# Two reorderings and a final norm summed over features on all partitions, in a one-core decoder layer

## Chip, cores and metric

The kernel runs on one core of a Trainium2 chip. The metric is the device time of one execution in microseconds; the median of three runs is given. The engines are named as in the profile: PE (TensorE, the matrix engine), DVE (the vector engine), ACT (the scalar engine), POOL (GpSimd) and SP, whose queue issues nearly all DMAs.

## What is computed

One layer of a hybrid decoder on 1,024 prompt tokens with 16 meta tokens ahead of them, and on 64 new tokens (8 sequences of 8): 1,104 columns in all, of which the 16 meta columns are dropped behind the attention. Everything is float32, width 1,024. Cut to what matters here:

```
u  = rmsnorm(h, norm_mix)
z  = u @ w_in + b_in                    # 48 tiles of 128 outputs
h += (gated sum of pooling, convolution and attention branches) @ w_out
u2 = rmsnorm(h, norm_mlp)
h += square(relu(u2 @ w_up)) @ w_down   # 1024 -> 4096 -> 1024
y  = rmsnorm(h, norm_final)

def _rmsnorm(x, g):
    y = x32 * lax.rsqrt(jnp.mean(x32 * x32, axis=-1, keepdims=True) + NORM_EPS)
    return y * g
```

The outputs are y and the new states of the three branches.

## The kernel before

Features lie on partitions (8 tiles of 128) and tokens on columns. Each float32 product is made of three matmuls in a faster type: both operands are split into a high part (ACT copies it: `whi`, `uh`, `oph`) and a low part (DVE subtracts: `wlo`, `ul`, `opl`), and high x high, high x low and low x high are summed in one PSUM bank. The engines' lists are written out by hand in Python order (`manual_schedule`): each engine runs its instructions in the order in which the code issues them, and waits for semaphores.

Three places matter.

**The head.** The columns of x come in three chunks `CH` of 416, 320 and 368 columns. The first five tiles of w_in (`NHEAD`) run their products on chunk 0 before the norm is known, and scale afterwards. `proj_mm(ti, ci)` is the product of tile ti on chunk ci, 24 matmuls into a bank from `pmain`; `proj_chunk(ti, ci, ps)` takes it out of the bank again (DVE `un`, L903, then ACT), which frees the bank. The sixth call of `pmain` uses the bank of the first. `norm1(ci)` is the norm of a chunk as six steps: steps 0 and 1 square (ACT, L304) and add (DVE, L306); step 2 sums over the features with one-column matmuls, which puts tokens on partitions (PE L260), takes the reciprocal root (`rstd_cols`: DVE, ACT, DVE) and makes diagonal matrices of it (DVE L266); step 3 broadcasts those diagonals to all partitions with a matmul (PE L271); steps 4 and 5 scale and split. n1 is that list for chunk 1, n2 for chunk 2.

**The seam.** The MLP's two products are done with a Strassen-like scheme: 16 pairs of up products with 7 steps each, then 7 down products (`NPROD`), each over 4 output pairs mp and 2 halves hf. Up results ca and cb leave the banks on DVE or ACT, are squared, combined (`op_steps`: the differences d) and stored to DRAM. `op_load(n, q)` loads operand q of down product n back (SP's queue; four buffers rotate), `op_split(n, q)` splits it into oph (ACT) and opl (DVE). Operands 0 to 3 are read by the first half hf = 0 of a down product's pairs, 4 to 7 by hf = 1. In the last up pair (j = 15), step i splits operand i; step 5 also splits the second piece of down weights (`W.split_to(2)`, then `W.flush()` for wlo). Step 6 of the up products writes the bank that step 4's cb empties.

**The tail.** The last down product runs over 288 and then 256 columns. `final(srcs, a, c, last)` is the last norm over columns a to c. With `last` it has three steps: f0 (sums with tokens on partitions, reciprocal root on 128x2, diagonals), pre (ACT scales two of the eight tiles by norm_final), f3 (broadcast, copy to SBUF, eight scaled outputs, stores).

Of the kernel before, what the change touches and what calls it, by code (L numbers as in the profile page):

```python
# [7 lines left out]
F32 = mybir.dt.float32  # L8
# [106 lines left out]
def hybrid_trunk_kernel(ctx, tc, I, O):  # L115
# [61 lines left out]
    one = pool.tile([P, 4], F32, name="one", tag="st", bufs=8)  # L177
    V.memset(one, 1.0)
    A.activation(one, one, AF.Sqrt)
    X = [[None] * 8 for _ in CH]  # L180

    def load_x(ci, k0=0, k1=8):
# [37 lines left out]
    def col(off):  # L220
        return vec[:, off:off + 1]
# [657 lines left out]
    def proj_mm(ti, ci):  # L879
        kind, j = TILES[ti]  # L880
        wh, wl = wts[ti][:2]
        a, c = CH[ci]
        if kind in "qz" and ci == 0:
            a = NM
        ps = pmain()
        mm3(ps[:, :c - a], wh, wl, [(k, (Uh[k][:, a:c], Ul[k][:, a:c])) for k in range(8)])
        return ps
# [206 lines left out]
    n2 = norm1(2)  # L1094
    proj_open(4)
    b0_.append(proj_mm(4, 0))
    n1[2]()
    n2[0]()
    n2[1]()
    proj_chunk(3, 0, b0_[3])  # L1100
    b1_ = [proj_mm(0, 1)]
    proj_chunk(4, 0, b0_[4])
    b1_.append(proj_mm(1, 1))
    n1[3]()
    n2[2]()
    b1_.append(proj_mm(2, 1))
    proj_chunk(0, 1, b1_[0])
    proj_chunk(1, 1, b1_[1])
    n2[3]()
# [434 lines left out]
    def op_load(n, q):  # L1544
        if n < NPROD:
            ld[n, q] = page2("ld")
            SP.dma_start(ld[n, q][:, :L], opD[DORD[n][1], q])

    def op_split(n, q):
        if n < NPROD:  # L1550
            t = ld.pop((n, q))
            h, l = BD[n, q] = page("oph", F32R), page("opl", F32R)
            split(h[:, :L], l[:, :L], t[:, :L])
# [27 lines left out]
    for s in range(7 * NPAIR):  # L1581
# [41 lines left out]
        if j == NPAIR - 1:  # L1623
            for n in range(2):
                BC.pop((BX[i], n))
            if i < 5:
                op_split(0, i)
                op_load(0, i + 2)
            elif i == 5:
                op_split(0, 5)  # L1630
                op_split(0, 6)
                op_load(1, 0)
                op_load(1, 1)
            if i == 1:
                W.split_to(1)
                W.flush()
            elif i == 4:
                W.load_to(3)
            elif i == 5:
                W.split_to(2)  # L1640
                W.flush()
# [80 lines left out]
    def final(srcs, a, c, last):  # L1722
# [25 lines left out]
        def pre(ms):  # L1748
            for m in ms:
                h = H[m][:, a:c]  # L1750
                A.activation(h, h, AF.Copy, scale=col(V_NF + m))

        def f3():
            b = px2()
            bcast_tokens(b, box["r"], w)
            s = page("fbc")
            A.activation(s[:, :w], b[:, :w], AF.Copy)
            t = [page("fo")[:, :4 * w].rearrange("p (m c) -> p m c", m=4) for _ in range(2)]
            for m in range(8):
                h, o = H[m][:, a:c], t[m // 4][:, m % 4]  # L1760
                if m in (2, 5):
                    G.tensor_tensor(o, h, s[:, :w], ALU.mult)
                else:
                    V.scalar_tensor_tensor(o, h, col(V_NF + m), b[:, :w], ALU.mult, ALU.mult)
                if m in (0, 1, 3, 5, 7):
                    n = 2 if m > 1 else 1
                    (A if m in (1, 5) else SP).dma_start(
                        O["y"][m + 1 - n:m + 1, :, a:c].rearrange("m p c -> p m c"),
                                 t[m // 4][:, m % 4 + 1 - n:m % 4 + 1])
        idle = lambda: None  # L1770
        if last:
            return [f0, lambda: pre((2, 5)), f3]
        return [f0, idle, idle, idle, f1, idle, idle] + [f2(m) for m in range(8)]

    WD = {}
# [1 line left out]
    for n in range(NPROD - 1):  # L1777
        for mp in range(4):
# [3 lines left out]
            for hf in range(2):  # L1782
# [2 lines left out]
                W.split_to(i + 2)  # L1785
                W.flush()
                q = 2 * mp + hf
                op_split(n + 1, q)
                if q < 6:
                    op_load(n + 1, q + 2)  # L1790
# [185 lines left out]
```

## Time and profile before

| | us |
|---|---|
| median of 3 runs (lowest, highest) | 1661.78 (1661.28, 1661.79) |
| the profiled execution | 1662.0 |
| its span, first to last instruction | 1660.1 |
| PE busy | 1642.7 (99%) |
| DVE busy | 1134.5 (68%) |
| ACT busy | 750.5 (45%) |
| POOL busy | 5.8 |
| moved by DMA | 250.78 MB, 151 GB/s on the mean |

Busy shares are of the span. A matmul's record is longer than the distance to the next one, since matmuls overlap; where the text counts matmuls, it goes by their starts. A float32 matmul of the norms (not split into three) leaves two records. "PEclk" is the share of TensorE's full clock that was granted: 1.00 is 2.4 GHz, 0.50 is 1.2 GHz.

### The profile page before, as it was taken

How to read it: one execution, taken by the hardware profiler on the slowest of the kernel's cores; microseconds unless marked ns; L12 is line 12 of the kernel's file. 1: busy time of each engine (PE TensorE's matmuls, PEld its weight loads, DVE VectorE, ACT ScalarE, POOL GpSimd, SP SyncE). 2: the span in 40 equal slices, each digit the busy share in tenths (PEclk: the TensorE clock that was granted, in tenths of full speed). 3: DMA queues.
4: the chain of work that ended last, by engine and by line, in shares of the span. 5: the costliest groups of instructions: out<-in, count | busy, mean ns of one | idle time of the engine just before them, and what ended most of it. 6: DMA issues, size and time to landing. Idle time of an engine off the chain costs nothing.

```text
span 1660.1 us, 28943 instructions
## 1 busy us (share of the span) xinstructions
PE 1642.7 (99%) x11568; PEld 1618.2 (97%) x11568; DVE 1134.5 (68%) x2120; ACT 750.5 (45%) x1428; POOL 5.8 (0%) x14
## 2 busy tenths in 40 slices
PE   9999999999999999999999999999999999999997
PEld 8999999999999999999999999999999999999997
DVE  7786767867776666455584687777777844457674
ACT  6537667467675342364243343233332533333341
POOL 0000000000000000000000000000000000000000
PEclk9999999999999999999999999999999999999998
DMA  6051221231225353344253447777776955556652
GB/s 207 15 110 52 71 79 42 68 77 41 81 63 173 97 197 113 104 184 146 80 172 124 152 162 242 244 237 246 243 241 227 323 194 184 183 184 222 204 173 85
DMA packets 132123, 250.78 MB, mean 151 GB/s; under 512 B 33459, under 2 KB 64148, under 8 KB 131988
## 3 DMA queue, kind: packets, MB, share of 16 engines
q1 hardware_dynamic: 131428, 248.45, 46.2%
q8 instruction: 91, 1.49, 0.4%
q10 hardware_dynamic: 560, 0.48, 0.1%
q14 instruction: 44, 0.36, 0.1%
HBM read 168.52 MB, written 80.36 MB: 150 GB/s over the span
## 4 chain that ended last, share of the span: by engine, by line
PE 95%; DVE 2%; ACT 1%; DMA 1%; issue 0%; SPq 0%; DVEq 0%; ACTq 0%
PE pm L151 13%; PE pm L153 13%; PE pm L152 13%; PE m L1663 7%; PE m L1665 7%; PE m L1667 7%; PE m L1470 6%; PE m L1473 6%; PE m L1472 6%; PE pn L151 3%; PE pn L153 3%; PE pn L152 3%; PE px L634 2%; PE px L622 2%; PE qk L581 2%; PE px L271 1%
## 5 line engine op out<-in xcount | busy, mean ns | idle before, releaser
L151 PE MATMUL pm<-uh,whi 128*128 128x320 f32 (+3 forms) x1008 | 338.5, 336 | 0.6 <-ACT uh L342 0.5
L153 PE MATMUL pm<-uh,wlo 128*128 128x320 f32 (+3 forms) x1008 | 333.1, 330 | 0.0
L152 PE MATMUL pm<-ul,whi 128*128 128x320 f32 (+3 forms) x1008 | 332.2, 330 | 0.6 <-DVE ul L343 0.6
L1663 PE MATMUL m<-oph,whi 128*128 128x272 f32 (+2 forms) x896 | 258.5, 289 | 0.0
L1665 PE MATMUL m<-opl,whi 128*128 128x272 f32 (+2 forms) x896 | 258.0, 288 | 0.0
L1667 PE MATMUL m<-oph,wlo 128*128 128x272 f32 (+2 forms) x896 | 257.8, 288 | 0.0
L93 ACT ACTIVATE whi<-wraw 128x1024 fp32r<-128x1024 f32 (+1 forms) x127 | 130.0, 1025 | 205.6 <-PE m L1665 138.3
L94 DVE TENSOR_TENSOR wlo<-wraw,whi 128x1024 fp32r<-128x1024 f32 (+1 forms) x127 | 150.6, 1187 | 98.3 <-ACT whi L93 98.3
L151 PEld LDWEIGHTS pm<-uh,whi 128*128 128x128 f32 x1008 | 190.8, 189 | 2.6 <-ACT uh L342 1.3
L152 PEld LDWEIGHTS pm<-ul,whi 128*128 128x128 f32 x1008 | 191.3, 190 | 1.9 <-DVE ul L343 1.5
L153 PEld LDWEIGHTS pm<-uh,wlo 128*128 128x128 f32 x1008 | 190.3, 189 | 0.4
L1665 PEld LDWEIGHTS m<-opl,whi 128*128 128x128 f32 x896 | 168.8, 188 | 0.0
L1663 PEld LDWEIGHTS m<-oph,whi 128*128 128x128 f32 x896 | 168.6, 188 | 0.0
L1667 PEld LDWEIGHTS m<-oph,wlo 128*128 128x128 f32 x896 | 168.5, 188 | 0.0
L456 DVE SCALAR_TENSOR_TENSOR y<-ext,vec,y 128x1024 f32<-128x1024 f32 x120 | 152.5, 1271 | 0.0
L1470 PE MATMUL m<-bch,wlo 128*128 128x272 f32 x448 | 129.2, 288 | 2.0 <-DVE cb L1614 2.0
L1470 PE MATMUL m<-bch,whi 128*128 128x272 f32 x448 | 129.3, 289 | 0.6 <-DVE h L1409 0.6
L1473 PE MATMUL m<-bch,whi 128*128 128x272 f32 x448 | 128.9, 288 | 0.0
L1473 PE MATMUL m<-bch,wlo 128*128 128x272 f32 x448 | 128.8, 288 | 0.0
L1472 PE MATMUL m<-bcl,whi 128*128 128x272 f32 x448 | 128.7, 287 | 0.0
L1472 PE MATMUL m<-bcl,wlo 128*128 128x272 f32 x448 | 128.7, 287 | 0.0
L1470 PEld LDWEIGHTS m<-bch,wlo 128*128 128x128 f32 x448 | 84.2, 188 | 2.2 <-issue 2.2
(364 smaller groups left out, 3418.1 us busy)
## 6 DMA issues: line engine op xcount, KB each, us to landing
wraw<-w_in SPq DMA_DIRECT2D x46, 512.0 KB, 3.9
opT<-d SPq DMA_DIRECT2D x64, 272.0 KB, 3.0
ld<-opT SPq DMA_DIRECT2D x32, 544.0 KB, 4.6
wd<-w_down SPq DMA_DIRECT2D x32, 512.0 KB, 5.8
sumD<-wd SPq DMA_DIRECT2D x32, 512.0 KB, 4.3
wraw<-sumD SPq DMA_DIRECT2D x32, 512.0 KB, 3.6
gt<-gD SPq DMA_DIRECT2D x24, 544.0 KB, 4.7
ld<-opB SPq DMA_DIRECT2D x23, 544.0 KB, 4.7
```

The lines of the kernel that those rows point to most:

```text
L93: self.nc.scalar.activation(hi, r, AF.Copy)
L94: self.late.append(lambda lo=lo, r=r, hi=hi: self.nc.vector.tensor_tensor(lo, r, hi.bitcast(F32), ALU.subtract))
L151: PE.matmul(ps, lhsT=wh[k], rhs=xh, start=first and i == 0, stop=False)
L152: PE.matmul(ps, lhsT=wh[k], rhs=xl, start=False, stop=False)
L153: PE.matmul(ps, lhsT=wl[k], rhs=xh, start=False, stop=last and i == n - 1)
L456: V.scalar_tensor_tensor(y[:, :NP], e[:, k:k + NP], w, y[:, :NP], ALU.mult, ALU.add)
L1470: PE.matmul(ps, lhsT=wh, rhs=xh, start=first and k == 0, stop=False, skip_group_check=True)
L1472: PE.matmul(ps, lhsT=wh, rhs=xl, start=False, stop=False, skip_group_check=True)
L1473: PE.matmul(ps, lhsT=wl, rhs=xh, start=False, stop=k == 3, skip_group_check=True)
L1663: PE.matmul(ps, lhsT=wh[:, w], rhs=xh[:, r], start=k == 0, stop=False, skip_group_check=True)
L1665: PE.matmul(ps, lhsT=wh[:, w], rhs=xl[:, r], start=False, stop=False, skip_group_check=True)
L1667: PE.matmul(ps, lhsT=wl[:, w], rhs=xh[:, r], start=False, stop=k == 15, skip_group_check=True)
```

## The change

It has three parts.

In the head, `proj_chunk(3, 0)` and the product of tile 0 on chunk 1 move ahead of n1's step 2 (sums of chunk 1) and the squares of chunk 2; the product of tile 2 on chunk 1 moves ahead of n1's step 3 (broadcast) and n2's step 2 (sums of chunk 2).

At the seam, the splits of operands 4, 5 and 6 of the first down product and the load (1, 1) move out of the last up pair into the first pass of the down loop, behind the get of the first weights and ahead of the split of operand (1, 0).

In the tail, the last 256 columns take their sums with a matmul of a full 128x128 matrix of ones (e0), so that every partition has the sums of all columns; the reciprocal root is then computed at 256 columns on all partitions by ACT and DVE. The diagonals, the broadcast and the copy to SBUF go.

```diff
+    epsc = pool.tile([P, 4], F32, name="epsc", tag="epsc")
+    V.memset(epsc, EPS)
...
     proj_open(4)
     b0_.append(proj_mm(4, 0))
+    proj_chunk(3, 0, b0_[3])
+    b1_ = [proj_mm(0, 1)]
     n1[2]()
     n2[0]()
     n2[1]()
-    proj_chunk(3, 0, b0_[3])
-    b1_ = [proj_mm(0, 1)]
     proj_chunk(4, 0, b0_[4])
     b1_.append(proj_mm(1, 1))
+    b1_.append(proj_mm(2, 1))
     n1[3]()
     n2[2]()
-    b1_.append(proj_mm(2, 1))
     proj_chunk(0, 1, b1_[0])
     proj_chunk(1, 1, b1_[1])
     n2[3]()
...
+            if i < 4:
+                op_split(0, i)
             if i < 5:
-                op_split(0, i)
                 op_load(0, i + 2)
             elif i == 5:
-                op_split(0, 5)
-                op_split(0, 6)
                 op_load(1, 0)
-                op_load(1, 1)
...
+        def e0():
+            b = box["b"] = px2()
+            for n, (src, off) in enumerate(srcs):
+                PE.matmul(b[:, :w], lhsT=ones, rhs=src[:, off:off + w], start=n == 0,
+                          stop=n == len(srcs) - 1)
+
         def f3():
-            b = px2()
-            bcast_tokens(b, box["r"], w)
-            s = page("fbc")
-            A.activation(s[:, :w], b[:, :w], AF.Copy)
+            p = page("fst")
+            v, s, y, u = (p[:, 256 * i:256 * i + w] for i in range(4))
+            b = box["b"][:, :w]
+            A.activation(s, b, AF.Sqrt, bias=epsc[:, :1], scale=1.0 / 1024)
+            V.tensor_scalar(v, b, 1.0 / 1024, EPS, ALU.mult, ALU.add)
+            pre((2, 5))
+            V.reciprocal(y, s)
+            V.tensor_tensor(u, y, y, ALU.mult)
+            V.scalar_tensor_tensor(u, u, -0.5, v, ALU.mult, ALU.mult)
+            V.scalar_tensor_tensor(s, u, 1.5, y, ALU.add, ALU.mult)
...
-                    G.tensor_tensor(o, h, s[:, :w], ALU.mult)
+                    G.tensor_tensor(o, h, s, ALU.mult)
                 else:
-                    V.scalar_tensor_tensor(o, h, col(V_NF + m), b[:, :w], ALU.mult, ALU.mult)
+                    V.scalar_tensor_tensor(o, h, col(V_NF + m), s, ALU.mult, ALU.mult)
...
         if last:
-            return [f0, lambda: pre((2, 5)), f3]
+            return [e0, f3]
...
                 q = 2 * mp + hf
+                if n == q == 0:
+                    op_split(0, 4)
+                    op_load(1, 1)
+                    op_split(0, 5)
+                    op_split(0, 6)
                 op_split(n + 1, q)
```

PE's list in the head, around the broadcast of chunk 1 (the first row with diag) and the sums of chunk 2 (st<-ones,sq). Before:

```order
L151 MATMUL pm<-uh_116,whi 128x320
L152 MATMUL pm<-ul_124,whi 128x320
L153 MATMUL pm<-uh_116,wlo 128x320
L271 MATMUL px<-diag,ones 128x128 x3
L260 MATMUL st_562<-ones,sq 128x1 x3
L151 MATMUL pn<-uh_109,whi 128x320
L152 MATMUL pn<-ul_117,whi 128x320
```

After, the same place:

```order
L151 MATMUL pn<-uh_118,whi 128x320
L152 MATMUL pn<-ul_126,whi 128x320
L153 MATMUL pn<-uh_118,wlo 128x320
L273 MATMUL px<-diag,ones 128x128 x3
L262 MATMUL st_589<-ones,sq 128x1 x3
L273 MATMUL px<-diag,ones 128x128 x3
L151 MATMUL pn<-uh_111,whi 128x320
```

The product of 24 matmuls that stood between the sums of chunk 2 and their broadcast (the second row with diag) now stands ahead of both.

DVE's list at the seam, from the cb that step 6 of the last up pair waits for. opl_13981, opl_14018 and opl_14022 are the low parts of operands 4, 5 and 6, wlo_14030 that of the second piece of down weights, the rows with d12 and d34 the differences of op_steps. Before:

```order
L1614 TENSOR_TENSOR cb_13787<-m2_13790,s15_13788 128x544
L157 TENSOR_TENSOR opl_13981<-ld_13912,oph_13980 128x1088
L999 TENSOR_TENSOR wd_13782<-wd_13782 128x512
L1618 TENSOR_TENSOR ca_13786<-m2_13991,s15_13788 128x544
L157 TENSOR_TENSOR opl_14018<-ld_13950,oph_14017 128x1088
L157 TENSOR_TENSOR opl_14022<-ld_13984,oph_14021 128x1088
L94 TENSOR_TENSOR wlo_14030<-wraw_13986,whi_14029 128x1024
L1477 SCALAR_TENSOR_TENSOR ca_13786<-ca_13786 128x1088
L157 TENSOR_TENSOR opl_13832<-ca_13786,oph_13831 128x544
L1477 SCALAR_TENSOR_TENSOR cb_13787<-cb_13787 128x1088
...
L1517 TENSOR_TENSOR d34_14066<-cb_13787,d12_14064 128x544
L157 TENSOR_TENSOR opl_14074<-ld_14025,oph_14073 128x1088
```

After, where opl_14062, opl_14068 and opl_14072 are those of operands 4, 5 and 6 and wlo_14018 that of the second piece of weights:

```order
L1616 TENSOR_TENSOR cb_13789<-m2_13792,s15_13790 128x544
L1001 TENSOR_TENSOR wd_13784<-wd_13784 128x512
L1620 TENSOR_TENSOR ca_13788<-m2_13989,s15_13790 128x544
L94 TENSOR_TENSOR wlo_14018<-wraw_13984,whi_14017 128x1024
L1479 SCALAR_TENSOR_TENSOR ca_13788<-ca_13788 128x1088
L157 TENSOR_TENSOR opl_13834<-ca_13788,oph_13833 128x544
L1479 SCALAR_TENSOR_TENSOR cb_13789<-cb_13789 128x1088
...
L1519 TENSOR_TENSOR d34_14054<-cb_13789,d12_14052 128x544
L157 TENSOR_TENSOR opl_14062<-ld_13914,oph_14061 128x1088
L157 TENSOR_TENSOR opl_14068<-ld_13952,oph_14067 128x1088
L157 TENSOR_TENSOR opl_14072<-ld_13982,oph_14071 128x1088
L157 TENSOR_TENSOR opl_14076<-ld_14015,oph_14075 128x1088
```

Three splits of operands moved from ahead of the weights' low part to behind the differences; ahead of cb nothing moved.

## Rows read from the trace of the kernel before

**Rows 1.** Page, busy us, share of the span, instructions of each engine.

```profile
PE 1642.7 (99%) x11568; PEld 1618.2 (97%) x11568; DVE 1134.5 (68%) x2120; ACT 750.5 (45%) x1428; POOL 5.8 (0%) x14
```

**Rows 2.** Waits of PE, whole span: us in total, times, longest.

```profile
PE m L1470 <- DVE cb L1614: 2.0, 1, 2.0
```

**Rows 3.** Windows: length, busy us (records) per engine, POOL, granted PEclk, DMA.

```profile
33.55:34.68 1.13, 0.00 (x1) 0.03 (x1) 1.03 (x3) 0.00 (x0) 0.00 (x0) 1.00 0.00 0
35.90:39.10 3.20, 3.20 (x13) 3.20 (x13) 2.29 (x10) 3.08 (x9) 0.00 (x0) 0.50 0.01 3
39.50:44.00 4.50, 4.50 (x32) 4.50 (x31) 3.90 (x8) 1.28 (x4) 0.00 (x0) 1.00 0.00 0
1300.97:1302.99 2.02, 0.01 (x1) 0.03 (x1) 2.02 (x4) 0.72 (x1) 0.00 (x0) 1.00 1.04 418
1303.00:1306.50 3.50, 3.50 (x28) 3.50 (x29) 3.50 (x5) 1.84 (x3) 0.00 (x0) 1.00 1.03 420
```

**Rows 4.** Timeline of the head's first stop: start, us, engine, line, instruction, idle before.

```profile
34.45 1.08 DVE L903 TENSOR_TENSOR un<-pm,rb 128x416 f32<-128x416 f32 x2
34.68 0.80 PE L260 MATMUL st<-ones,sq 128*128 128x1 f32 x6 [1.13 <-DVE sq L306]
35.34 0.39 PE L151 MATMUL pm<-uh,whi 128*128 128x320 f32 x1
```

**Rows 5.** Timeline: additions, sums and diagonals of chunk 2, next product.

```profile
38.53 4.41 DVE L306 TENSOR_TENSOR sq<-sq 128x368 f32<-128x368 f32 x7
44.70 0.73 PE L260 MATMUL st<-ones,sq 128*128 128x1 f32 x6
45.29 0.39 PE L151 MATMUL pn<-uh,whi 128*128 128x320 f32 x1
46.70 0.68 DVE L266 TENSOR_SCALAR diag<-ident,st 128x128 f32<-128x128 f32 x3
```

**Rows 6.** Timelines of DVE, ACT and PE at the seam.

```profile
1302.13 0.72 DVE L1614 TENSOR_TENSOR cb<-m,s 128x544 f32<-128x544 f32 x1
1304.57 0.72 DVE L1618 TENSOR_TENSOR ca<-m,s 128x544 f32<-128x544 f32 x1
1307.60 1.22 DVE L94 TENSOR_TENSOR wlo<-wraw,whi 128x1024 fp32r<-128x1024 f32 x1
1315.26 1.29 DVE L157 TENSOR_TENSOR opl<-ld,oph 128x1088 fp32r<-128x1088 f32 x1
...
1306.16 1.06 ACT L93 ACTIVATE whi<-wraw 128x1024 fp32r<-128x1024 f32 x1
...
1312.18 0.29 PE L1665 MATMUL m<-opl,whi 128*128 128x272 f32 x1
```

**Rows 7.** Loads of down weights, 1296 to 1312: issue (ns, first and last), landing.

```profile
L64 SPq DMA_DIRECT2D wraw<-w_down x2: 333/494/654, 1298.2 to 1299.8; - x2
...
DMA to landing us min/median/max: 7.6/7.7/7.8
```

**Rows 8.** Timeline of the tail.

```profile
1649.29 0.38 PE L1731 MATMUL px<-ones,fsq 128*128 128x1 f32 x2 [1.31 <-ACT fsq L1837]
...
1653.46 2.44 DVE L1764 SCALAR_TENSOR_TENSOR fo<-h,vec,px 128x256 f32<-128x256 f32 x6 [1.60 <-ACT fbc L1757]
```

**Rows 9.** Groups by line and shape: busy us, mean ns of one, idle before.

```profile
L1441 DVE RECIPROCAL mv<-mv 128x9 f32<-128x9 f32 x1 | 0.2, 214 | 0.0
...
L751 DVE RECIPROCAL ssm<-ssm 128x1 f32<-128x1 f32 x8 | 1.3, 164 | 0.3
...
L1167 DVE TENSOR_TENSOR gt<-gt 128x256 f32<-128x256 f32 x8 | 3.4, 425 | 0.3
...
L1751 ACT ACTIVATE h<-h,vec 128x256 f32<-128x256 f32 x2 | 0.9, 492 | 0.0
```

**Rows 10.** Timeline: a float32 matmul of ones at 384 columns.

```profile
665.52 0.81 PE L508 MATMUL px<-lacc,ones 128*128 128x384 f32 x2
```

## Prediction

> **What bounds the kernel now.** I read the page's busy times first: TensorE (PE) is busy for 99% of the span, the vector engine (DVE) for 68%, the scalar engine (ACT) for 45% [rows 1]. So the time is the length of one queue of matrix products plus the few places where that queue stands still, plus the tail after the last product. Any work of DVE or ACT costs nothing unless PE waits for it. I then read who PE waits for: the longest single wait is 2.0 us, for DVE's cb at the end of the MLP's up products [rows 2]. Third, I read windows around each stop for the granted clock: the first stop, 1.13 us at 33.55, is followed from 35.90 to 39.10 by a clock of 0.50, the 1.2 GHz level, while after the 2.02 us stop at 1300.97 the clock was 1.00 in every later row that I read [rows 3]. A stop can thus cost twice: once as idle time and once as slow products behind it. Between the two stops of rows 3 the head differs in one thing: the stop at 33.55 runs on into six one-column products, 0.80 us of almost no work [rows 4].
>
> The change has three parts in three stages: the head (the order of norm sums and products), the seam between the up and down products (when three operands are split), and the last norm.
>
> **The head, first stop.** Before, PE waits for the sums of squares of chunk 1 until 34.68, runs the one-column products (sums1), and starts the product of tile 0, chunk 1 at 35.34 [rows 4]. After, that product stands ahead of sums1. It does not start at 33.55, though: it writes the PSUM bank that proj_chunk(0, 0) frees, and the DVE instruction that frees it (the first of the two `un`, which together take 1.08 us from 34.45) still stands behind the same squares. The first ends near 35.05. So PE waits until about 35.08: a gain of 35.34 - 35.08 = 0.26, and sums1 are paid behind the product, at their start-to-start cost of 45.29 - 44.70 = 0.59 as for chunk 2 [rows 5]. Net +0.3.
>
> **The head, second stop.** Before, the sums of chunk 2 are followed by a whole product of 24 matmuls, and only then by the broadcast of their result. The order of after puts broadcast 1, sums 2 and broadcast 2 directly behind one another on PE. Between sums 2 and broadcast 2 lies the chain DVE, ACT, DVE that turns sums into a diagonal. In before it runs, with nothing else on DVE, from 44.70 (sums) to the diagonals that start at 46.70 and take 0.68 for three [rows 5]. PE is free at 45.29 and could start the first broadcast near 47.05, when the first of the three diagonals (0.23 each, and a hand-over) is written. What hid this was the product; its cover is gone, and PE, whose list has nothing else to run there, stands for 47.05 - 45.29 = 1.75 us. Are the sums there in time? Their seven additions took 4.41 [rows 5]; in after they start behind the diagonals, 47.38 - 45.43 = 1.95 after the end of sums1, and so end 6.4 after it, while PE has two products of 24 x 0.141 = 3.4 each (the rate of 39.50 to 44.00 [rows 3]) and a broadcast to run before it wants them: 6.8 and more. They are hidden, by half a microsecond or a little over. The other moves in the head (one `un` ahead of the chain on DVE, squares of chunk 2 later on ACT) have the same cover.
>
> The clock in the head: before, 13 records fit into the 3.20 us at 0.50, where 32 took 4.50 at 1.00 [rows 3], so the fall cost 3.20 - 13 x 0.141 = 1.4 us. After, the first stop is longer (1.5) but ends in full products; the second has broadcast and one-column sums around it, as the stop had that brought the fall before. I expect one fall, at one of the two: no change. Ends: -1.4 (none) and +1.4 (both). The head is +0.3 + 1.75 = +2.1.
>
> **The seam.** The 2.02 us stop stays: DVE's cb, for which PE waits, has the same instructions ahead of it as before; the three splits taken away stood behind it. DVE is in order and without a pause there, so cb still starts at 1302.13 [rows 6]. Behind it, before, DVE ran: split 4, a sum, ca at 1304.57, splits 5 and 6, then the low half of the next weights (wlo) at 1307.60. After, a sum, ca and at once wlo. But wlo needs whi from ACT, which began at 1306.16 and took 1.06; its weights were issued at 1298.2 and took 7.6 us to land, so it can't begin before 1305.8 [rows 6, 7]. DVE therefore stands still from about 1304.0 to 1307.25 and wins just 0.35 on before. The rest, from wlo to the last difference of op_steps, is the same list: 1315.26 - 0.35 = 1314.91 is when the first of the four splits now put there (operand 4) starts; it takes 1.29 as in before. It is done at 1316.2. PE's second half of the first down product, the first reader of operand 4, has as its second matmul, the first to read the low part, the one at 1312.18 [rows 6]. So PE stands for 1316.2 - 1312.2 = **4.0 us**. Operands 5 and 6 follow at 1.2 each, faster than the 1.5 that PE takes for one (12 matmuls at 3.50 / 28 = 0.125 [rows 3]): no further wait.
>
> What is queued behind: SP's queue. The load (1, 1) now stands behind two stores and waits for the buffer of split 4, until 1316.2, and (1, 2) behind it for that of split 5; the next load of weights goes out behind both, at about 1318. With the 7.7 us of rows 7 it lands at 1325.8; PE, delayed by 4, needs those weights split at 1328.1. Just hidden; the price if not is below.
>
> Clock: the stop is twice the longest that left the clock at 1.00 [rows 3], so I count one fall behind it, 1.4 as in the head. Bounds: 0, and 2.8 if the fall lasts twice as long. The seam is +4.0 + 1.4 = +5.4.
>
> **The last norm.** Before, from the ready square at 1649.29 to the first scaled output at 1653.46 it takes 4.17 [rows 8]. After, with 256 columns on all partitions:
> - one product of 256 columns (the other, of facc, runs ahead). The like at 384 columns took 0.81 [rows 10]; two records of a third fewer columns give 0.60. At the lower clock about 1.0.
> - ACT's Sqrt from PSUM with a bias from a tile: 0.49, as the scaled copy at 256 columns [rows 9]. DVE's v runs beside it.
> - DVE's reciprocal at 256 columns, which no row shows: 164 ns at 1 column and 214 at 9 [rows 9], 6.25 ns a column, gives 0.164 + 255 x 0.00625 = 1.76. The lower bound is the ordinary rate, 0.43 (the tensor product of 256); the upper bound 2.3, a third above the slope. I take 1.76, since the two rows are of this very operation.
> - three DVE steps of 0.43 (same row) and five hand-overs of 0.02: 1.4.
>
> Sum 0.60 + 0.49 + 1.76 + 1.4 = 4.25: +0.1, with ends at -1.25 and +1.0. The six outputs and the stores behind are as before. (The Trainium skill, in "VectorE: DVE Perf Modes", section "First, the fixed hardware budget", says that Reciprocal uses an iterative divide with a repeat count of 8; at the 0.96 GHz that the page gives, 8 cycles a column would be an estimate of 2.1 us, and the tail would lose 0.5 rather than 0.1. The slope of rows 9 speaks for a little less.)
>
> **Sum.** +2.1 + 5.4 + 0.1 = +7.6. The profiled run took 1662.0 (span 1660.1), 0.2 above the median of 1661.78. Forecast 1661.8 + 7.6 = **1669.4**.
>
> **Rivals.**
> 1. The clock is kind: no fall at the seam, or none in the head. For it: the 2.02 us stop at full clock. Against: the 4 us are double that. With neither: 1669.4 - 2.8 = 1666.6; with one, 1668.0.
> 2. Not slower: DVE doesn't stand still at the seam. If whi were ready when ca is done, 1304.0, because the weights land 2 to 3 us earlier than before (the loads of operands behind them now wait longer), the standstill of 1304.0 to 1307.25 goes, split 4 ends near 1313.0, the stop shrinks to 0.8 and the clock stays: 1661.8 + 2.1 + 0.8 + 0.1 = 1664.8, by 0.18% not told from no change. It decides at whi's start: by 1304 instead of 1306.16. Against it: what is ahead of these weights in SP's queue is unchanged, and so should be their 7.6 us [rows 7]. For a gain the head's fall would have to vanish too and the reciprocal go at the ordinary rate: 1664.8 - 1.4 - 1.35 - 0.8 = 1661.2.
> 3. SP's queue bites: the weights held back on SP come late, by 1 to 2 us, and a second stop follows six to twelve us behind the first: 1671.4.
>
> **How the numbers follow.** Forecast 60%, kind clock 17%, DVE without the standstill 12%, late weights 11%. The range reaches from the kind clock with the tail's lower end (1666.6 - 1.25 = 1665.4) to late weights with some of the tail's upper end (1672.0). A measurement of this kernel can tell about 0.2%, 3.3 us, from no change. Slower by more than that is the forecast, the kind clock and the late weights: 0.87. Within it is most of rival 2: 0.10. Faster 0.03.
>
> **What would show it.** On PE a wait of about 1.75 at some 49 us for the diagonals, and one of about 4 for opl in the first down product; DVE idle for 3 us ahead of wlo with ACT's whi as its releaser; the granted clock at 0.50 behind the second; a reciprocal of 1.4 to 2.3 us in the tail. I am wrong if PE shows no wait for opl, if the stop for cb is gone too, or if the first stop shrinks below 1.1 us.

## The result, and the profile after

| | before | after |
|---|---|---|
| median, us (lowest, highest; executions) | 1661.78 (1661.28, 1662.65; 4) | 1671.92 (1671.11, 1672.95; 4) |
| the profiled execution, us | 1662.0 | 1671.11 |
| its span, us | 1660.1 | 1669.0 |

The ratio is 1.0061, with a 95% interval of 1.0043 to 1.0078: slower by 7 to 13 us. The forecast was 1669.4 with a range of 1665.4 to 1672.0. The sign and the mechanism came as forecast; the size came out 2.5 us above the forecast and 0.1 below the upper end of the range, and the sections below say which terms were too small.

Whom PE waits for in the kernel after (us in total, times, longest):

```profile
PE m L1665 <- DVE opl L157: 4.4, 1, 4.4
PE m L1472 <- DVE cb L1616: 2.0, 1, 2.0
PE px L273 <- DVE diag L268: 1.7, 1, 1.7
...
PE pm L151 <- DVE un L905: 1.5, 1, 1.5
```

Beside [rows 2] this is the forecast read off directly: the wait for cb is still there and still 2.0, and a wait for opl, more than twice as long, has come behind it. The line for the diagonals has a twin in the kernel before, at 1651.81, which is another wait: that of the last norm, which the change does away with.

```profile
PE px L271 <- DVE diag L266: 1.7, 1, 1.7
```

The two stops of the head can be seen in PE's timeline (start, us, engine, line, instruction, idle before):

```profile
35.19 0.41 PE L151 MATMUL pm<-uh,whi 128*128 128x320 f32 x1 [1.54 <-DVE un L905]
...
38.81 0.73 PE L262 MATMUL st<-ones,sq 128*128 128x1 f32 x6
...
49.65 0.91 PE L273 MATMUL px<-diag,ones 128*128 128x128 f32 x6 [1.70 <-DVE diag L268]
```

The first is the 1.13 of [rows 4], now 1.54 and waiting for `un` instead of the squares; the second, 1.70 for the diagonals, has no counterpart in the head of the kernel before, where a product lay there [rows 5]. The granted clock in windows (columns as in [rows 3]) behind the two stops, and around the one at the seam:

```profile
36.00:46.00 10.00, 10.00 (x72) 10.00 (x71) 5.90 (x17) 5.05 (x12) 0.00 (x0) 1.00 0.01 2
47.90:49.60 1.70, 0.05 (x1) 0.00 (x0) 1.20 (x7) 0.20 (x1) 0.00 (x0) 1.00 0.11 31
50.40:60.00 9.60, 9.60 (x66) 9.60 (x65) 9.13 (x19) 5.36 (x11) 0.00 (x0) 1.00 0.00 0
1313.50:1317.90 4.40, 0.29 (x2) 0.08 (x1) 4.37 (x6) 3.79 (x4) 0.00 (x0) 0.97 0.00 0
1317.90:1321.00 3.10, 2.78 (x12) 2.78 (x13) 3.10 (x4) 0.00 (x0) 0.00 (x0) 0.50 0.59 181
1322.00:1332.00 10.00, 10.00 (x81) 10.00 (x81) 4.54 (x4) 3.85 (x5) 0.00 (x0) 1.00 0.97 372
```

Neither stop of the head is followed by slow products in this execution: the clock is 1.00 in 36 to 46 and in 50.4 to 60, where the kernel before had 0.50 from 35.90 to 39.10 [rows 3]. The stop at the seam is: 0.50, the 1.2 GHz level, from 1317.9 to about 1321.

The seam on DVE, ACT and PE, to be read beside [rows 6]:

```profile
1303.42 0.72 DVE L1616 TENSOR_TENSOR cb<-m,s 128x544 f32<-128x544 f32 x1
...
1309.22 1.23 DVE L94 TENSOR_TENSOR wlo<-wraw,whi 128x1024 fp32r<-128x1024 f32 x1 [3.85 <-ACT whi L93]
...
1316.88 4.89 DVE L157 TENSOR_TENSOR opl<-ld,oph 128x1088 fp32r<-128x1088 f32 x4
```

```profile
1308.13 1.06 ACT L93 ACTIVATE whi<-wraw 128x1024 fp32r<-128x1024 f32 x1 [10.16 <-DMA wraw<-w_down]
```

```profile
1304.29 0.37 PE L1472 MATMUL m<-bch,wlo 128*128 128x272 f32 x1 [2.02 <-DVE cb L1616]
...
1318.22 0.59 PE L1665 MATMUL m<-opl,whi 128*128 128x272 f32 x1 [4.43 <-DVE opl L157]
```

DVE stands still for 3.85 us ahead of wlo, because ACT's whi waits for its weights; the four splits of operands start only behind everything else, at 1316.88, and PE waits 4.43 us for the first. The weights took 8.3 us to land (issues from 1296 to 1312: KB each, median us to landing), where [rows 7] had 7.6 to 7.8:

```profile
wraw<-w_down SPq DMA_DIRECT2D x2, 512.0 KB, 8.3
```

The tail, in the order of time, to be read beside [rows 8]:

```profile
1656.51 0.70 PE L1757 MATMUL px<-fsq,ones 128*128 128x256 f32 x2 [0.99 <-ACT fsq L1855]
```

```profile
1657.25 0.47 ACT L1764 ACTIVATE fst<-px,epsc 128x256 f32<-128x256 f32 x1 [0.79 <-PE px L1757]
```

```profile
1657.75 0.42 DVE L1765 TENSOR_SCALAR fst<-px 128x256 f32<-128x256 f32 x1 [1.74 <-ACT fst L1764]
1658.09 1.74 DVE L1767 RECIPROCAL fst<-fst 128x256 f32<-128x256 f32 x1
...
1661.25 3.40 DVE L1777 SCALAR_TENSOR_TENSOR fo<-h,vec,fst 128x256 f32<-128x256 f32 x6
```

From the square's product to the first output it takes 1661.25 - 1656.51 = 4.74 us (before 4.17), and the six outputs take 3.40 (before 2.44).

**Where the 8.9 us of span come from.** PE goes on behind cb at 1304.29, against 1302.99 in the kernel before: +1.3 up to there. That is the head, and it is less than its two stops cost, because this execution of after has no slow products there and that of before has. From there to the last square on DVE it takes 350.83 us (to 1655.12), against 344.91 (1302.99 to 1647.90): +5.92 for the seam. By the starts of matmuls, which is how the prediction counted, the stop is 4.74 of it: the matmul that waits for opl starts 13.93 us behind the restart (1304.29 to 1318.22), where before it was 9.19 (1302.99 to 1312.18 [rows 6]). (The idle time of 4.43 is shorter, since it counts from the end of the record ahead, and records overlap.) The slow products are most of the other 1.2. The rest, 1.7, is the tail.

### The profile page after: what moved, and what is told of

Read it like the earlier page. It is cut to its first block, busy times and chain, and to the rows that moved or that the text cites. A ratio compares the mean times of both kernels' runs of the same rounds, so it can differ in the third digit from the quotient of the medians.

```text
span 1669.0 us, 28922 instructions
## 1 busy us (share of the span) xinstructions
PE 1641.5 (98%) x11560; PEld 1616.1 (97%) x11560; DVE 1137.5 (68%) x2119; ACT 750.4 (45%) x1427; POOL 6.1 (0%) x14
## 4 chain that ended last, share of the span: by engine, by line
PE 94%; DVE 2%; DMA 2%; ACT 1%; SPq 0%; issue 0%; DVEq 0%; ACTq 0%
PE pm L151 12%; PE pm L153 12%; PE pm L152 12%; PE m L1665 7%; PE m L1663 7%; PE m L1667 7%; PE m L1472 6%; PE m L1475 6%; PE m L1474 6%; PE pn L151 3%; PE pn L153 3%; PE pn L152 3%; PE px L636 2%; PE px L624 2%; PE qk L583 2%; PE px L273 1%
```

## Experiments

Each kernel below was timed beside the kernel before on the same chip, in three sets on two chips; the kernel before had medians of 1661.88 (29 executions), 1661.62 (27) and 1661.98 (33). There the executions of one kernel spread over some 5 us, more than in the runs of the result, so two readings stand beside each ratio. One is the trace. The other uses that every execution comes with its span and its mean granted clock: among the 89 executions of the kernel before, the mean span is 1658.3 at a clock of 0.997 (33 of them), 1659.9 at 0.996 (21), 1660.5 at 0.995 (30) and 1663.0 at 0.994 (5). Much of the spread is thus the number of slow stretches that an execution happened to have. Span times clock takes these out: it is called the full-clock length below, 1653.1, 1652.8 and 1652.8 for the kernel before in the three sets, and what it misses of the span (6.9, 6.5 and 6.8) is called the loss to the clock.

Not all of that loss is time lost. The clock is 0.50 over the last 7 to 11 us of every one of the 14 traces (before, after and the twelve kernels below) too, where PE has next to nothing left to run. The trace of the kernel before shows it, and also a slow stretch at 8.5 us, ahead of the one of [rows 3]:

```profile
8.50:11.80 3.30, 3.12 (x9) 2.82 (x9) 3.20 (x7) 3.08 (x7) 0.00 (x0) 0.50 1.07 399
1650.30:1660.10 9.80, 1.20 (x4) 0.93 (x4) 3.59 (x13) 1.39 (x4) 1.41 (x2) 0.50 0.33 110
```

The end alone makes 3 to 5 us of the loss in each execution. So only the difference between two kernels' losses says something; a longer end counts for about half in the full-clock length; and the clock of an execution is given to 0.001, which is 1.7 us, so that only means over many executions can be compared.

### Each part alone

Head alone (the reordering of `proj_mm` and of the steps of n1 and n2 as in the change, nothing else), seam alone, tail alone.

> Only the head of the change. Theory from the trace after: the two stops cost net +0.3 (first) and +1.7 (second), and the slow products that followed the first stop before, 1.4 us, don't come back because the stop no longer runs on into one-column products: +0.6, with PE stops near 1.5 for un and 1.7 for diag and a granted clock of 1.00 from 35 to 60 us. Rival, that a fall comes somewhere in the head all the same in most executions: +2.1, and a stretch at 0.50.

> Only the seam of the change. Theory: PE waits 4.0 to 4.5 us for opl and one fall of the clock behind it costs 1.4 to 1.5: +5.4 to +5.9. Rival, that the fall at the seam came only because the one in the head had gone (one fall in each execution, wherever): the stop alone, +4.0 to +4.5, with no stretch at 0.50 behind it.

> Only the last norm of the change. Theory from the trace after: 0.57 later to the first scaled output (v waits for the Sqrt since both lie in one tile) and 0.96 more for the six outputs: +1.5 to +1.7. Rival, as the prediction had it: the chain costs the same as before, +0.1, and what looked like 1.7 in the tail of after is the lower clock or the chance of one execution.

| kernel | ratio, 95% interval | us on before, by the ratio | full-clock length on before | loss to the clock |
|---|---|---|---|---|
| head alone | 1.0023 (1.0015 to 1.0032) | +3.8 | +2.7 | 8.7 |
| seam alone | 1.0026 (1.0013 to 1.0038) | +4.3 | +3.8 | 8.0 |
| tail alone | 1.0014 (1.0005 to 1.0023) | +2.3 | +2.0 | 6.9 |

The three ratios add up to +10.4, the change gave 10.1: as far as the intervals tell, the parts simply add, and each of them makes the kernel slower.

Head alone: the two stops are those of after, but behind the second the clock is low in this execution. PE's windows behind the stop for the diagonals, and some 940 us later, where PE has no stop at all:

```profile
50.20:54.00 3.80, 3.80 (x18) 3.80 (x19) 3.73 (x10) 2.43 (x5) 0.00 (x0) 0.60 0.00 0
```

```profile
994.00:996.00 2.00, 2.00 (x10) 2.00 (x10) 2.00 (x9) 0.00 (x0) 0.00 (x0) 0.50 0.48 180
```

So the theory of the expectation (no fall in the head any more) falls, and its rival is nearer, though +2.1 is below the interval's +2.5: the second stop brings a fall in some executions and not in others. The loss to the clock, 8.7 against 6.9 (a difference of 1.7, give or take 1.0), says on the mean one fall more than before.

Seam alone: the stop is 3.45, the fall behind it is there, and DVE's pause ahead of wlo is shorter, since the weights landed in 7.2 us.

```profile
1304.55 1.23 DVE L94 TENSOR_TENSOR wlo<-wraw,whi 128x1024 fp32r<-128x1024 f32 x1 [2.71 <-ACT whi L93]
```

```profile
1313.55 0.59 PE L1663 MATMUL m<-opl,whi 128*128 128x272 f32 x1 [3.45 <-DVE opl L157]
```

```profile
1313.60:1317.00 3.40, 3.40 (x16) 3.40 (x17) 3.40 (x3) 0.07 (x1) 0.00 (x0) 0.53 0.73 189
```

The head's order is that of before here, and its stop was not followed by a fall in this execution either, so the fall at the seam is not one that moved over from the head on every run. From PE's restart behind cb (1300.75) to the last square (1650.57) it takes 349.82, 4.91 more than before. By starts 3.61 of that is the stop (1300.75 to 1313.55 is 12.80, against 9.19), and most of the other 1.3 the slow products. Pause, landing and stop by starts go together: 3.85, 8.3 and 4.74 in after, 2.71, 7.2 and 3.61 here, about 1.1 less each.

Tail alone: 1647.20 to 1651.94 from the square's product to the first output, 4.74, and 3.40 for the six outputs, the same to 0.01 as in after. That is 1.5 more than before, inside the interval of +0.8 to +3.8, which leaves out the rival's +0.1: the rival (that this was chance) falls.

### The seam: what makes the stop

**Earlier weights.** The seam of the change, the second piece of down weights in a buffer of its own and loaded at step 0:

```diff
-                                  n == mp == hf == 0 or
+                                  n == mp == 0 or
...
-            W.load_to(1)
+            W.load_to(2)
```

> The seam of the change, but with a buffer of its own for the second piece of down weights, loaded several us earlier, so that its high half is done before DVE wants it. Theory, that DVE's standstill ahead of wlo is what makes the stop long: DVE goes on from ca to wlo without a pause, the wait of PE for opl falls from 4.4 to about 0.8 to 1.2, the clock stays at 1.00, and the time is 4 to 5 below that of the seam alone, +0.8 to +1.2 on the kernel before. Rival, that the three splits themselves, 3.7 us of DVE work put ahead of a reader that wants them at once, make it: the wait stays above 3, and the time within 1.5 us of the seam alone.

The ratio is 1.0019 (1.0010 to 1.0027): +3.1. PE's two waits, and DVE's pause where the earlier loads push back one of an operand:

```profile
1303.88 0.37 PE L1470 MATMUL m<-bch,wlo 128*128 128x272 f32 x1 [2.86 <-DVE cb L1614]
...
1314.22 0.39 PE L1663 MATMUL m<-opl,whi 128*128 128x272 f32 x1 [0.95 <-DVE opl L157]
```

```profile
1290.16 1.29 DVE L157 TENSOR_TENSOR opl<-ld,oph 128x1088 fp32r<-128x1088 f32 x1 [4.34 <-ACT oph L156]
```

The pause ahead of wlo is gone, the wait for opl is 0.95 instead of 3.45, and there is no fall behind it: what makes the stop long is the standstill, as the theory had it. This is also rival 2 of the prediction, made to happen, which priced the stop at 0.8. The time is 1.2 below that of the seam alone, not 4 to 5. The wait for cb grew by 0.86, since DVE waited 4.34 for an operand's load where it had waited 3.06 in the seam alone:

```profile
1287.03 1.29 DVE L157 TENSOR_TENSOR opl<-ld,oph 128x1088 fp32r<-128x1088 f32 x1 [3.06 <-ACT oph L156]
```

By the starts of PE's matmuls the seam is 2.7 longer here than in the kernel before: 0.4 at a short wait at 1291.75, 0.84 at cb, 1.15 at opl and the rest in small steps behind. So the earlier load cured one wait and made others.

**The stop filled.** The seam of the change with products whose results are thrown away ahead of the one that waits:

```diff
+                if n == 0 and q == 1:
+                    fill = px2()
+                    for _ in range(26):
+                        PE.matmul(fill[:, :272], lhsT=WD[0, 0, 1][0][:, :P],
+                                  rhs=BD[0, 4][0][:, :272], start=True, stop=True)
                 dprod(n, mp, hf, b, TWO)
```

> The seam of the change with 26 products of 272 columns (some 3.2 us at full clock, results thrown away) put into the stop of 3.5 us, ahead of the product that waits for opl. Theory, that the slow stretch behind the stop comes from PE's standing still: with the stop filled the granted clock stays at 1.00 through the down products, and the time is about 1 to 1.5 below that of the seam alone, +3.5 on the kernel before. Rival, that the fall has another cause (the change of kind of work, or chance): it comes in as many executions as with the seam alone, and the time is the same or, by the fillers that overrun the wait, slower.

The ratio is 1.0019 (1.0010 to 1.0028), and the loss to the clock 6.2 us against 8.0 for the seam alone. PE, and the clock behind the fillers:

```profile
1311.77 3.37 PE L1806 MATMUL px<-oph,whi 128*128 128x272 f32 x26
```

```profile
1316.20 0.40 PE L1663 MATMUL m<-opl,whi 128*128 128x272 f32 x1 [0.93 <-DVE opl L157]
```

```profile
1318.00:1328.00 10.00, 10.00 (x82) 10.00 (x81) 5.98 (x6) 3.80 (x4) 0.00 (x0) 1.00 0.96 332
```

The work that PE could not do is as late as before (3.2 of fillers and 0.93 of wait), but nothing slow follows. From the restart behind cb (1302.70) to the last square (1651.75) it takes 349.05, 4.14 more than in the kernel before: all of it fillers and wait. In the traces the theory holds: with PE busy in the stop no fall came, where it came behind 2 of 2 stops left empty. On the mean of the executions it is not shown: by the ratios the gain on the seam alone is 1.2, within intervals that overlap, and the 1.8 by the loss to the clock, from 6 and 11 executions, is not clear of noise either.

**The opposite edit.** In the kernel before, the splits of operands 0 to 4 one step later, away from the cb that PE waits for:

```diff
+            if 0 < i < 5:
+                op_split(0, i - 1)
             if i < 5:
-                op_split(0, i)
                 op_load(0, i + 2)
             elif i == 5:
+                op_split(0, 4)
                 op_split(0, 5)
```

> The opposite edit at the seam on the kernel before: in the last up pair the splits of operands 0 to 4 run one step later, so that one split fewer (1.2 us of DVE) stands ahead of the cb for which PE waits 2.0. Theory, that cb is late only because of the DVE work ahead of it: the wait falls to about 0.8, with no new wait for opl in the first down product, -1.2. Rival, that the split comes back as a wait for opl behind it, as in the change: the two waits together stay at 2.0 or above, no gain.

The ratio is 0.9990 (0.9981 to 0.9999), -1.6 by it and by the medians: a little faster than the kernel before. The wait for cb does not shrink to 0.8, it is gone, and a shorter one has come for the low half of the third piece of weights:

```profile
1316.03 0.39 PE L1669 MATMUL m<-oph,wlo 128*128 128x272 f32 x1 [1.23 <-DVE wlo L94]
```

So the rival was right in kind (DVE's delay comes back later, as a wait for the weights' low half and not for opl), but not in size: 1.23 for 2.02.

**That, and the wait that took its place.** As before this, and the split of operand (1, 0) behind that low half:

```diff
-                op_split(n + 1, q)
-                if q < 6:
+                if n == 0 and q < 2:
+                    if q == 1:
+                        op_split(1, 0)
+                        op_load(1, 2)
+                        op_split(1, 1)
+                        op_load(1, 3)
+                else:
+                    op_split(n + 1, q)
+                if n == 0 and q < 2:
+                    pass
+                elif q < 6:
```

> The kernel before with the splits of operands 0 to 4 one step later, and the split of operand (1, 0) behind the low half of the third piece of down weights rather than ahead of it. Theory: the wait of 2.0 for cb is gone as in the run with the later splits alone, and the wait of 1.2 for wlo, which took its place there, goes too, since one split (1.2 us of DVE) less stands ahead of it: -2.5 to -3 on the kernel before. Rival, that the weights' low half waits for its landing rather than for DVE: the 1.2 stays, and the time is that of the later splits alone, -1.3 to -1.6.

```profile
1318.71 0.39 PE L1669 MATMUL m<-oph,wlo 128*128 128x272 f32 x1 [0.16 <-DVE wlo L94]
```

The ratio is 0.9987 (0.9978 to 0.9996): -2.2, and -2.5 by the medians (1659.48). The wait for cb, 2.02 in the kernel before, is gone, and of the one for the low half 0.16 is left. This version beats both kernels, by moving splits of operands out of DVE's way at two places where somebody waits; the change moved three of them to right ahead of their reader.

### The head: which of the two moves

**The first move alone** (`proj_chunk(3, 0)` and tile 0's product ahead of the sums of chunk 1; tile 2's product stays where it was):

```diff
+    proj_chunk(3, 0, b0_[3])
+    b1_ = [proj_mm(0, 1)]
     n1[2]()
     n2[0]()
     n2[1]()
-    proj_chunk(3, 0, b0_[3])
-    b1_ = [proj_mm(0, 1)]
```

> Of the head only the first move, the product of tile 0 on chunk 1 ahead of the sums; the product of tile 2 stays between the sums of chunk 2 and their broadcast, as in the kernel before. Theory, that the second stop is due to that product's move alone: no wait for diag near 49 us, and what is left is the first stop, 1.5 for un and +0.3 in all, within 0.1% of the kernel before. Rival, that the sums of chunk 2, started later, bring a stop of their own behind broadcast 1: a wait of 0.5 to 2 for sq, +0.8 to +2.3.

The ratio is 1.0030 (1.0019 to 1.0042): +5.0, no better than the whole head. The theory falls. PE's two stops, DVE's additions for the second, and the clock behind it:

```profile
34.92 0.42 PE L151 MATMUL pm<-uh,whi 128*128 128x320 f32 x1 [1.58 <-DVE un L903]
...
45.62 1.39 PE L260 MATMUL st<-ones,sq 128*128 128x1 f32 x6 [2.01 <-DVE sq L306]
```

```profile
41.16 4.41 DVE L306 TENSOR_TENSOR sq<-sq 128x368 f32<-128x368 f32 x7
```

```profile
45.60:49.00 3.40, 3.38 (x14) 3.38 (x15) 1.99 (x10) 1.16 (x3) 0.00 (x0) 0.52 0.08 20
49.00:53.00 4.00, 4.00 (x18) 4.00 (x17) 0.76 (x2) 1.01 (x2) 0.00 (x0) 0.56 0.00 0
```

With the sums of chunk 1 one product later, the seven additions of chunk 2 end near 45.5, and PE, with one product fewer ahead of them, wants their result at 43.6. Two falls follow one another. That is the rival's stop, 2.01, at its upper end; by the full-clock length it comes to +2.6, and the loss to the clock, 9.4, is the largest of all kernels here.

**The second move alone** (tile 2's product ahead of broadcast 1):

```diff
+    b1_.append(proj_mm(2, 1))
     n1[3]()
     n2[2]()
-    b1_.append(proj_mm(2, 1))
```

> Of the head only the second move: the product of tile 2 ahead of broadcast 1 and the sums of chunk 2; the first stop stays as in the kernel before. Theory, that each of the two moves pays for a stop by itself, since the product moved was the cover of either the sums or of the chain behind them: a wait of 1.7 for diag near 49 us and about +1.7 to +2. Rival, from the first move alone having cost 2.0 by a wait for sq: that it is the first move that makes all of the head's loss, and the second alone costs nothing or wins.

The ratio is 1.0019 (1.0010 to 1.0028), +3.1; the full-clock length is +1.6, and the loss to the clock 8.3. The stop at the diagonals is the forecast 1.70, and in this execution a fall stands behind it:

```profile
47.89 1.62 PE L271 MATMUL px<-diag,ones 128*128 128x128 f32 x6 [1.70 <-DVE diag L266]
```

```profile
47.90:51.30 3.40, 3.40 (x15) 3.40 (x16) 2.71 (x8) 2.04 (x4) 0.00 (x0) 0.54 0.00 0
```

So each move costs a stop by itself, 2.0 or 1.7. Together they cost one of the two only (beside the 0.4 by which the first stop is longer), since the second move gives the additions the product that the first has taken from them, and takes it from the chain behind the sums.

### The tail: what was mis-sized

**v in its own tile.** The tail alone, with this edit:

```diff
-            v, s, y, u = (p[:, 256 * i:256 * i + w] for i in range(4))
+            s, y, u = (p[:, 256 * i:256 * i + w] for i in range(3))
+            v = page("fv")[:, :w]
```

> The tail of the change, with v in a tile of its own. Theory, that v waited for ACT's Sqrt only because both wrote the tile fst: v now runs beside the Sqrt, the reciprocal starts about 0.35 earlier behind the ready square, and the way from the square's product to the first scaled output is 4.4 instead of 4.74. Rival, that what orders them is the shared source in PSUM: v stays behind the Sqrt, 4.74. The six outputs stay at 3.4 either way.

```profile
1650.54 0.42 DVE L1767 TENSOR_SCALAR fv<-px 128x256 f32<-128x256 f32 x1 [1.75 <-ACT fst L1766]
```

The theory falls: v writes another tile now and still starts behind the Sqrt, 4.74 in all; the ratio is 1.0013 (1.0003 to 1.0022), that of the tail alone. What the two instructions share is what they read, the bank px. The runs show that they go one after the other, not whether the chip could have run them side by side.

**The scale back in PSUM.** As above, and the last step writes px, which DVE's outputs read; ACT copies it to SBUF for POOL:

```diff
-            V.scalar_tensor_tensor(s, u, 1.5, y, ALU.add, ALU.mult)
+            V.scalar_tensor_tensor(b, u, 1.5, y, ALU.add, ALU.mult)
+            g = page("fg")[:, :w]
+            A.activation(g, b, AF.Copy)
```

> As with v in its own tile, and besides the final scale is written to PSUM, where DVE's six outputs read it as in the kernel before, while ACT copies it to SBUF for POOL's two. Theory, that the outputs went from 475 to 631 ns each because all three operands of theirs now lie in SBUF, beside POOL: they return to about 475, 2.44 for six, and the end comes about 1 us earlier than with v alone. Rival, that they are slow for another reason, such as the lower clock or the stores: they stay near 631 and the end does not move.

DVE's six outputs (duration in ns, min, median, max, first and last start): in after, and in this kernel.

```profile
L1777 DVE SCALAR_TENSOR_TENSOR fo<-h,vec,fst x6: 471/478/947, 1661.2 to 1664.2; 128x256 f32<-128x256 f32 x6
```

```profile
L1781 DVE SCALAR_TENSOR_TENSOR fo<-h,vec,px x6: 475/476/481, 1657.5 to 1659.5; 128x256 f32<-128x256 f32 x6
```

The median is 478 in after too; at a mean of 631 for the six that leaves two of about 940, and these make the 3.40. With the factor in PSUM none is above 481, and the six take 2.44. But the first of them waits for ACT's copy of the same bank:

```profile
1657.49 2.44 DVE L1781 SCALAR_TENSOR_TENSOR fo<-h,vec,px 128x256 f32<-128x256 f32 x6 [0.45 <-ACT fg L1774]
```

It is DVE behind ACT on one bank again. Of the 0.96 won 0.45 is given back, and what is left, 0.5, is too little for the time to show: 1.0010 (1.0000 to 1.0020).

**No POOL.** The tail alone, with `G.tensor_tensor` of the two tiles as `V.tensor_tensor`:

> The last norm of the change with POOL's two scaled tiles given to DVE. Theory, that two of DVE's six outputs took twice their time because POOL read and wrote SBUF beside them: all eight now take about 0.43 to 0.48, some 3.5 for eight, about the 3.4 that six took, and the time is that of the tail of the change within 0.3 us. Rival, that the first outputs are slow for what stands ahead of them (the stores, the first touch of a tile): two of eight still take 0.94, 4.4 in all, +1 on the tail of the change.

```profile
L1778 DVE SCALAR_TENSOR_TENSOR fo<-h,vec,fst x6: 475/478/484, 1653.7 to 1656.4; 128x256 f32<-128x256 f32 x6
```

All operands are in SBUF, as in the change, and no output is slow once POOL stands still: the eight run from 1653.71 on in 3.13. The ratio is 1.0008 (0.9999 to 1.0017). The theory holds. It takes both, a DVE instruction with two tensors in SBUF and a POOL instruction beside it. POOL's two show it from the other side, in the kernel before and in after:

```profile
L1762 POOL TENSOR_TENSOR fo<-h,fbc x2: 726/726/727, 1653.5 to 1654.2; 128x256 f32<-128x256 f32 x2
```

```profile
L1775 POOL TENSOR_TENSOR fo<-h,fst x2: 880/890/899, 1661.4 to 1662.3; 128x256 f32<-128x256 f32 x2
```

## Why the prediction was right in sign and short in size

**The head's stops: right.** 1.53 was forecast for the first (until 35.08 from 33.55) and 1.54 came; 1.75 for the second, and 1.70 came. From the start of the first stop to tile 3's product on chunk 1 it takes 16.66 us in after (33.65 to 50.31) and 14.40 with the head of before and no fall (seam alone, 32.86 to 47.26): +2.26, where the steps gave +2.05. That the sums' additions would be hidden "by half a microsecond or a little over" held in the change (they ended at 46.29 and PE wanted them at 47.22), and the first move alone showed how near it was. The full-clock length of the head alone is +2.7; of the 0.4 beyond 2.26 the trace shows only that most of it gathers in steps of 0.1 between 190 and 300 us, and its cause stays open.

**The head's clock: the step was wrong in kind.** It took the one fall of [rows 3] for a property of the place (the six one-column products) and expected "one fall, at one of the two: no change". With the head's first part as in before there are 11 profiled executions, the kernel before among them, and a fall stands behind the first stop in 5. Where a product waits for `un` instead (after, head alone, first move alone) it stands there in none of 3; behind the second stop, of 1.7 or 2.0, in 3 of 4. Whether a fall comes in the head thus differs from execution to execution in both kernels, and the profiled ones happen to show it in before and not in after. What the change does is to add a place where it may come. On the mean the loss to the clock is 8.7 for the head alone and 6.9 for the kernel before: about one fall more, where the step had none. Its price for the fall, 1.4, was a little low as well: it counted 32 records in 4.50 us, among them such as began ahead of the window, and by starts the fall of before cost 1.5 (15.94 from 33.55 to 49.49, against the 14.40).

**The seam's stop: the mechanism right, a term short by 0.7.** Every link came as told: cb kept its 2.02, DVE stood still ahead of wlo with ACT's whi as its releaser, the splits came behind the differences, the second matmul of the second half waited, and there was no further wait. The term that was short is the landing of the weights: 7.6 was taken from [rows 7], and 8.3 came in after, 7.2 in the seam alone; the stop went along, by starts 4.74 and 3.61 around the forecast 4.0. A landing read from one execution should have carried such a spread.

**The seam's clock: right.** One fall was forecast, at 1.4. It came, at 1.2 to 1.5 by starts, in both kernels whose stop was left long (3.45 and 4.43 of idle time) and not in the two where the stop was cut to 0.95 or filled; that is one execution of each.

**The tail: two terms missed, 1.3 of the 1.5.** The reciprocal was right (1.76 forecast from the slope of [rows 9], 1.74 measured). The product, from its start to the Sqrt, was 0.14 short. The steps that failed are "DVE's v runs beside it", which cost 0.34, and "The six outputs and the stores behind are as before", which cost 0.96. For the first the row was on record and was passed over: in [rows 8] the first output, which reads px and not fbc, waits 1.60 for ACT's copy of px to fbc. DVE had stood behind ACT on a shared bank already. The Trainium skill says so in "PSUM — Partial Sum Buffer", section "PSUM bank collisions raise a hardware error": the compiler's scheduler adds a dependency between any two instructions on different engines that touch the same bank and the same quarter of the partitions, reads too; the traces here, where both engines read all partitions, agree, with the 0.34 or 0.35 of v in five kernels and the 0.45 of the outputs. For the second, the Trainium skill's "SBUF — State Buffer", section "Who interferes with whom", says that a DVE instruction with two SBUF inputs contends with a GpSimd instruction that reads SBUF. The traces agree: up to 947 ns beside POOL, 478 without it, 476 with one operand in PSUM. The change turned an operand from PSUM to SBUF, and the prediction passed over that as no change of cost.

**The sum.** At full clock the parts alone came to 2.7, 3.8 and 2.0, where 2.05, 4.0 and 0.1 had been forecast; the clock cost about 2 us more than in before (8.8 lost per execution of after, of which there are four, against 6.5 to 6.9), where 1.4 had been. That makes some 10.5 against 7.55; the change itself, on fewer executions, gave 10.1. Most of the gap is the tail. That the time still fell inside the range is in part luck: the upper end had been drawn mostly for late weights with a second stop, which did not come, and the tail's outputs, which had been put at no change, and the clock filled that place.

**The rivals.** The kind clock did not come as a case: falls vary between executions and the median goes by their mean. The late weights did not bring a second stop. DVE without the standstill was made by hand and left a stop of 0.95, near its price of 0.8, with the clock at 1.00 behind it.

## What to carry to other kernels

An operation moved off one engine's busy stretch is free only if its reader is far away: before moving it, look for the first reader on the engine that sets the time, and for what stands ahead of it in the new place, loads included. If an operand is moved from PSUM to SBUF, or computed with two engines from one PSUM bank, price it again, with what POOL and ACT do at that moment. A slow stretch seen behind one short stop in one trace is a chance and not a term with a sign; several executions have to be read before it is put into a sum.

## What the runs showed of the hardware

- A stop of PE is paid for twice only sometimes. In 14 profiled executions a slow stretch stood behind 5 of 11 stops of 1.13 to 1.17 us in the head, 2 of 12 waits for cb of 1.66 to 2.86 us, 3 of 4 stops of 1.7 to 2.0 us between the broadcasts of the head, and 2 of 2 stops of 3.45 and 4.43 us. In four of them, one of which is shown above, a slow stretch came between 990 and 998 us, where PE was busy throughout, and in seven between 8 and 15 us.
- In a slow stretch the granted clock was 0.50; one among full products cost 1.2 to 1.5 us by the starts of matmuls.
- DVE's reciprocal took 1744 ns at 256 columns, with 164 at 1 and 214 at 9 [rows 9]: a straight line, 6.2 ns a column.
- An instruction of DVE with two tensor operands in SBUF took up to 947 ns beside a POOL instruction that reads SBUF and 478 alone; the same with one operand in PSUM took 476 beside POOL.
